# Rotation tables queued behind low weight parts and traced later, state-space and first score products a turn or two later, and the norms' rows loaded a unit ahead, in a one-core hybrid decoder step

## The chip, the cores and the metric

The kernel runs on one core of one Trainium2 chip. The number that counts is the device time of one execution in microseconds (us). Each kernel is timed as the median of several runs.

A core has five engines with queues of their own: PE (TensorE, matmuls; its weight loads are listed as PEld), DVE (VectorE), ACT (ScalarE), POOL (GpSimd) and SP (SyncE, which here only issues DMAs). Each engine works through its own list of instructions in the order in which the program put them there. Engines wait for each other by semaphores, and an instruction that waits holds up everything behind it in its own list.

## The reference, cut to what matters

One layer of a decoder: 528 prompt tokens (16 meta tokens and 512 more) and 8 sample tokens go through the same weights, in float32.

```python
xn = rmsnorm(x, norm_gain)
h = xn @ w_in                                  # 2048 x 8704
q, k, v, z_a, u, z_s, g_a, g_s = split(h)
q, k = rope(rmsnorm(q)), rope(rmsnorm(k))      # 16 query heads, 4 key heads of 64
o_a = sink_attention(q, k, v)                  # window 128, 16 meta keys, a sink
lam_bar = exp(lam * dt)                        # S5: complex diagonal, 64 groups x 64 states
b_bar = (lam_bar - 1) / lam * (b_re + i b_im)
h_t = lam_bar * h_(t-1) + b_bar u_t            # scan over time
y = gelu(Re(c h) + d_skip * u)
y = y * sigmoid(y @ w_glu + b_glu)
x + (sigmoid(g_a) * ((o_a * silu(z_a)) @ w_attn_out)
     + sigmoid(g_s) * ((y * silu(z_s)) @ w_ssm_out)) @ w_out
```

The new key and value windows and the final states are returned too.

## The kernel before, in words

**Weights.** A float32 product is made of three passes with shortened operands. Every weight tile `raw` of 128x1024 is loaded by SP, cut by ACT into a high part `whi` and by DVE into a low part `wlo = raw - whi`. PE then multiplies `whi` by the high and by the low part of the activations, and `wlo` by the high part. A low part that is late therefore stops PE.

**Stages, in the order of PE.** First come nine blocks of the input projection, taken as plain products (`mm`, line 1172). Sixteen quads follow: `Quads` and `quad` form two output blocks from seven products instead of eight, on sums and differences of weight tiles (`raw`, line 1077) and of activations (`tau`), with their products at line 1395 and their low parts at line 1079. A quad ends with DVE adding the last bank at line 1445. Quads 9 to 12, counted from 0, give the query heads. They go through `heads`, which writes each head block to DRAM as it is and with swapped halves (`rawD`, ten DMAs a quad). Then come the blocks listed in `ORDER1` (keys, values and the state-space input `u`), the rest of the gates, two plain stages (`w_glu` and the state-space output), the attention output, and eight quads for `w_out`.

**What runs beside them.** `Background` holds generators in three lanes. After a few matmuls the tracing code calls `step(budget)`. A generator then runs on to its next `yield`. `yield c` charges a cost `c` against the budget, and `yield None` ends that lane's turn. So a larger cost, or one more `yield None`, means that what follows is traced later in the program. In the quads a step comes after each of the seven products, with a budget of 0.5 (`GBUDGET`).

**What sets an engine's order.** The program is traced in one order, and a list scheduler then places each instruction on its engine by a model of its own. A low-priority instruction that looks ready early in that model may be placed well ahead of where it was traced. `with tc.issue_after(ins)` forbids this: every instruction traced inside it *on the engine of `ins`* comes after `ins`. `later()` is `issue_after(bg.last)`, where `bg.last` is the last product's final matmul. It binds the PE instructions traced inside and leaves DVE ones free.

**The rotation tables.** `ssm_prep` computes from `a`, `b` and `dt` on POOL some 200 small instructions (powers of the discretised eigenvalues, tables `T6` and `T11`). Then for each of eight unit blocks DVE makes a table out of `T11` and `T6` by four multiplications (line 308) and two combinations (lines 310 and 311), in one working buffer (`work`, the program's `room`). SP writes it to DRAM in two halves (`tabD`, line 314). The first two multiplications of the next table overwrite the half that is being written out, so they wait until those DMAs have landed.

**The state-space blocks.** `ssm_consts` loads and scales one block's constants and forms its `kp` products (line 410). `ssm_block` forms the `bu` products (line 471), scans on DVE, and forms the output products (lines 527 and 530).

**Norms of the heads.** `head_norms` takes the sums of squares that `heads` wrote to DRAM (`skD`, `sqD`), turns them into reciprocal roots on DVE and writes them back (`rkD`, `rqD`). `normed` lets the attention generator start, which also stands in lane 0 behind the eight state-space blocks.

**Attention.** It runs beside the last gates and the two plain stages: values, keys, then for each of four key heads the queries (`QT`, line 793) and four blocks of scores (line 809), softmax, transposes and weighing (line 858). The sample tokens' part ends at line 928, and `split` (lines 1678 and 1679) makes `A2` of it, which the attention output multiplies.

Of the kernel before, what the change touches and what calls it, by code (L numbers as in the profile page):

```python
# [146 lines left out]
    return r  # L147


def ssm_prep(nc, K, tmp, psum, dram, R, ident, a_prm, later, room):  # L150

    v = OnPool(nc, tmp)
    prm = K["prm"]
# [12 lines left out]
    v_.reciprocal(out=m2, in_=m2)  # L166
    dt = tmp.tile([P, 32], F32, name="dt")
    acc_exp(v, tmp, dt, ldt, 32)
    yield 1.6
    x = tmp.tile([P, 32], F32, name="xr")  # L170
    v.tensor_tensor(out=x, in0=are, in1=dt, op=ALU.mult)
    rho = tmp.tile([P, 32], F32, name="rho")
    acc_exp(v, tmp, rho, x, 32)
    th = tmp.tile([P, 32], F32, name="th")
    v.tensor_tensor(out=th, in0=aim, in1=dt, op=ALU.mult)
    yield 1.6

    magic = 12582912.0
    n = tmp.tile([P, 2, 32], F32, name="sc_n")
# [27 lines left out]
    v.tensor_tensor(out=e1, in0=r, in1=s, op=ALU.mult)  # L207
    lam = K["lam"]
    v.tensor_tensor(out=lam, in0=e1, in1=bc(rho, 1, 2), op=ALU.mult)
    yield 1.6  # L210

    g = tmp.tile([P, 2, 32], F32, name="f_g")
    v.tensor_scalar(out=g[:, 0], in0=lam[:, 0], scalar1=1.0, scalar2=None, op0=ALU.subtract)
# [13 lines left out]
    cmul(v, tmp, fv[:, :, 1:4], bc(fv[:, :, 0], 2, 3), lamp[:, 0, 0:3], lamp[:, 1, 0:3], (3, 32), "c96_")  # L227
    nF = K["nF"]
    v.tensor_scalar(out=nF, in0=fv[:, :, 0], scalar1=-1.0, scalar2=None, op0=ALU.mult)
    yield 1.3  # L230

    r4 = K["r4"]
    v.tensor_tensor(out=r4, in0=rho, in1=rho, op=ALU.mult)
# [12 lines left out]
    def powers(tab, z, cnt, tag):  # L246

        v.memset(tab[:, 0, :, 0], 1.0)
        v.memset(tab[:, 1, :, 0], 0.0)
        zs = [z]  # L250
        for i in range(3):
            nz = tmp.tile([P, 2, 32], F32, name=f"{tag}z{i}")
            cmul(v, tmp, nz, zs[-1], zs[-1][:, 0], zs[-1][:, 1], (32,), "c32_")
            zs.append(nz)
        n = 1
        for zp in zs:
            m = min(n, cnt - n)
            if m <= 0:
                break
            cmul(v, tmp, tab[:, :, :, n:n + m], tab[:, :, :, 0:m],  # L260
                 bc(zp[:, 0], 2, m), bc(zp[:, 1], 2, m), (32, m), "ct")
            n += m
            yield 0.8
        norm(tab, (32, cnt), "nt")
        yield 1.0
        return zs

    z = e1
# [13 lines left out]
    norm(c2, (32,), "n32")  # L282
    car = K["car"]
    v.tensor_tensor(out=car, in0=c2, in1=bc(r4, 1, 2), op=ALU.mult)
    yield 0.5
    for _ in range(14):
        yield None
    ft = psum.tile([P, 512], F32, name="tr")
    fts = tmp.tile([P, 2, P], F32, name="fts")
# [12 lines left out]
    t = [f.rearrange("p (r a i j) -> p r a i j", r=2, a=4, j=6) for f in (room[:, 0:8 * L], room[:, 8 * L:16 * L])]  # L302
    for ub in range(8):
        ps = slice(4 * ub, 4 * ub + 4)
        with later():
            for r in range(2):
                for e in range(2):
                    v_.tensor_tensor(out=t[r][:, e], in0=bc(T11[:, e, ps], 3, 6), in1=bc(T6[:, r, ps], 2, 11), op=ALU.mult)
            a, b = (f.rearrange("p r a i j -> p r (a i j)") for f in t)
            v_.tensor_tensor(out=a[:, 0], in0=a[:, 0], in1=b[:, 1], op=ALU.subtract)  # L310
            v_.scalar_tensor_tensor(out=a[:, 1], in0=a[:, 1], scalar=-1.0, in1=b[:, 0], op0=ALU.mult, op1=ALU.subtract)
            d = R["tabD"][ub].rearrange("p (x r l) -> p x r l", r=2, l=L)
            for r in range(2):
                nc.sync.dma_start(out=d[:, :, r], in_=t[0].rearrange("p r a i j -> p (r a) (i j)"))
        yield 2.4
# [23 lines left out]
def ssm_consts(nc, pool, dram, R, D, ub, a_bT, a_bN, a_cT, e32, d_skip, later, free):  # L339
# [64 lines left out]
    yield None  # L404

    kp = R["kp"]
    with later():
        for a in range(4):
            for i in range(2):
                nc.tensor.matmul(kp[32 * a:32 * a + 32, 0:P], lhsT=bb[:, a, i], rhs=CL[:, a, i, 0:4],  # L410
                                 start=(i == 0), stop=(i == 1))
# [34 lines left out]
def ssm_block(nc, pool, R, D, ub, y_out, later):  # L446
# [11 lines left out]
    tab = D["tab"]  # L458

    bu = R["bu"]  # L460

    def place(h, i, e):
        if (h, i) == (1, 0):
# [474 lines left out]
BUDGET2, BUDGET3, BUDGET4 = 6.0, 3.4, 4.8  # L938
HIGH = 4000
NLOAD = 3  # L940
NDELAY = 1
ATTC = (("kg", 1), ("kgs", 1), ("qg", 1), ("qgs", 1), ("mown", P), ("mprev", P), ("bd64", 4), ("sink", 16))
NXR = 10
NWARM = 9
# [85 lines left out]
class Quads:  # L1030
# [29 lines left out]
    def make(self, r):  # L1060
        nc = self.nc
        q, s = divmod(r, 7)
        if self.LOADS[s] is not None:
            self.load(4 * q + self.LOADS[s] + 4)
        if r < 7 and self.fourth:
            s = (0, 1, 2, 5, 3, 4, 6)[s]
        t = self.raw[4 * q + self.SRC[s]]
        pool, bufs = (self.pool, 3) if r % (3 + self.mp) < 3 else (self.more, self.mp)
        hi = pool.tile([P, 8, P], F32R, name="whi", bufs=bufs)
        lo = pool.tile([P, 8, P], F32R, name="wlo", bufs=bufs)  # L1070
        with self.tc.high_priority(offset=HIGH):
            for oi in self.SUMS[s]:
                if r < 7 and self.fourth and oi == (2, 0):
                    nc.gpsimd.dma_start(out=self.raw[2], in_=self.w[self.first], accum_op=ALU.add)
                    continue
                o, i = (self.raw[4 * q + j] for j in oi)
                nc.vector.tensor_tensor(out=o, in0=o, in1=i, op=ALU.add)  # L1077
            nc.scalar.copy(out=hi, in_=t)  # L1078
            nc.vector.tensor_tensor(out=lo, in0=t, in1=hi.bitcast(F32), op=ALU.subtract)  # L1079
        self.parts[r] = hi, lo  # L1080

    def upto(self, n):
# [10 lines left out]
def trunk(tc, A, O):  # L1093
# [62 lines left out]
        yield  # L1156


    pend, normed = [], []

    def mm(n, hi_of, lo_of, w0, budget=None, after=None, pool=None, name=None):

        ps = pool.tile([P, 2, 512], F32, name=name) if pool else mmp.tile([P, 2, 512], F32, name="mm")
        W = CH - w0
        for h in range(n):
            wh, wl = ws.get()
            for k in range(8):
                kt = 8 * h + k
                first, last = kt == 0, kt == 8 * n - 1
                for (wt, xo, f, l) in ((wh, hi_of, first, False), (wh, lo_of, False, False), (wl, hi_of, False, last)):  # L1170
                    for c in range(2):
                        m = nc.tensor.matmul(ps[:, c, 0:W], lhsT=wt[:, k], rhs=xo(kt, c), start=f, stop=l)  # L1172
                if k % grain[0] == grain[0] - 1:
                    bg.last = m.ins
                    bg.after = (ws.dve,) if at is not None else ()
                    bg.step((bud[0] if budget is None else budget) * grain[0] / 8)
            while pend and h == 0:
                pend.pop(0)()
            if after:
                after(h)  # L1180
        return ps[:, :, 0:W]
# [190 lines left out]
            pend.append(sums)  # L1372

    def head_norms():
        for src, dst, p, n in ((skD, rkD, 67, 32), (sqD, rqD, P, 65)):
            r1 = ev.tile([p, n], F32, name="z")
            r2 = ev.tile([p, n], F32, name="z")
            flat2 = lambda t: t.rearrange("a b -> (a b)").rearrange("(p n) -> p n", n=n)
            nc.sync.dma_start(out=r1, in_=flat2(src))
            v.tensor_scalar(out=r1, in0=r1, scalar1=1.0 / 64, scalar2=1e-6, op0=ALU.mult, op1=ALU.add)  # L1380
            rsqrt_dve(nc, ev, r2, r1, [p, n], "t", "")
            nc.sync.dma_start(out=flat2(dst), in_=r2)

    smp = []

# [113 lines left out]
    def xpart(k, c):  # L1499
# [4 lines left out]
    S = {}  # L1504
    flats = [xp.tile([P, 8 * CH], F32, name="work", tag=n) for n in ("xhq", "xlq")]
    bg.add(ssm_prep(nc, kept(flats[0][:, 0:NMADE], MADE), Places([flats[1], flats[0][:, NMADE:]], spots()), aux, dram, S,
                    C["idn"], A["prm"], lambda: tc.issue_after(bg.last), flats[1]))
    kD = dram.tile([P, NKEPT], F32, name="kept")

    def again():  # L1510
# [60 lines left out]
    for n_, (kind, n) in enumerate(ORDER1):  # L1571
# [4 lines left out]
        if kind == "h":  # L1576
            heads(n)
            if n == 3:
                pend.extend((head_norms, lambda: normed.append(1)))
            continue  # L1580
        if sp is None:
            spool = tc.tile_pool(name="ssm", bufs=2, side="right")
# [392 lines left out]
```

## Time and profile before

| | us |
|---|---|
| median of 3 runs | 1309.17 (1308.14 to 1310.37) |
| the profiled execution's own time | 1310.21 |
| its span in the profile | 1308.4 |
| PE busy | 1251.1 (96%) |
| DVE busy | 977.7 (75%) |
| ACT busy | 632.4 (48%) |
| POOL busy | 216.1 (17%) |

The granted TensorE clock was 0.986 on average over the span. HBM moved 226.75 MB, 173 GB/s on average. A row of the list of waits says which engine and line stood still, for what, for how long in total, how often, and how long at most. A row of the timeline gives start, duration, engine, line, operation, and in brackets the idle time before it with what ended that.

### The profile page before, as it was taken

What the parts mean: (1) busy time and instruction counts of PE and PEld (TensorE: products, weight loads), DVE (VectorE), ACT (ScalarE), POOL (GpSimd) and SP (SyncE); (2) the same over time, 40 slices, a digit from 0 to 9 for tenths busy, and PEclk for the clock granted to TensorE, in tenths of its full rate; (3) what the DMA queues carried; (4) which work ended last, traced back from release to release, by engine and by line L of the source; (5) the groups of instructions that cost most, each with busy time, mean ns of one, the idle gap of its engine ahead of it and who ended that gap; (6) DMA issues with size and microseconds to landing.
All of it is one profiled execution on the core that took longest, in us unless ns stands there. A gap on an engine that the chain in (4) does not pass through costs nothing.

```text
span 1308.4 us, 26458 instructions
## 1 busy us (share of the span) xinstructions
PE 1251.1 (96%) x10333; PEld 1226.8 (94%) x10333; DVE 977.7 (75%) x1516; ACT 632.4 (48%) x1351; POOL 216.1 (17%) x437
## 2 busy tenths in 40 slices
PE   9999982989999999999999998999999999999998
PEld 9999982979999999999999998989999999999998
DVE  8587843879778765777888857898995557787875
ACT  8553530435453539656653233667666323343442
POOL 0004997000000012222322122120010000000000
PEclk9999995999999999999999998999999999999999
DMA  8554331775355447666656479676676565464441
GB/s 286 196 172 147 116 128 30 153 177 153 128 160 162 149 144 225 186 201 182 176 158 185 123 223 258 187 246 212 191 229 219 188 202 181 147 220 153 154 138 50
DMA packets 125728, 226.75 MB, mean 173 GB/s; under 512 B 38700, under 2 KB 64260, under 8 KB 125572
## 3 DMA queue, kind: packets, MB, share of 16 engines
q1 hardware_dynamic: 116964, 206.63, 51.7%
q0 software_dynamic: 8640, 18.45, 5.7%
q8 instruction: 81, 1.33, 0.4%
q14 instruction: 43, 0.35, 0.1%
HBM read 185.34 MB, written 40.59 MB: 173 GB/s over the span
## 4 chain that ended last, share of the span: by engine, by line
PE 63%; DMA 12%; DVE 9%; POOL 8%; ACT 5%; issue 3%; SPq 2%; DVEq 0%; ACTq 0%; POOLq 0%
PE mm L1172 31%; PE pr L1395 27%; DMA tabD<-work 3%; ACT ct L362 2%; DMA xr<-in_x 1%; PE wg L858 1%; DMA sbw<-rawD 1%; DVE wlo L1013 1%; DMA c<-in_cT 1%; DMA raw<-in_w 1%; DMA bN<-in_bN 1%; POOL work L63 1%; ACT whi L1012 1%; POOL work L62 1%; POOL work L75 1%
## 5 line engine op out<-in xcount | busy, mean ns | idle before, releaser
L1078 ACT CAST whi<-raw 128x1024 fp32r<-128x1024 f32 x168 | 173.1, 1048 | 204.3 <-DVE raw L1077 121.0
L1079 DVE TENSOR_TENSOR wlo<-raw,whi 128x1024 fp32r<-128x1024 f32 x168 | 202.7, 1225 | 62.3 <-ACT whi L1078 61.9
L1395 PE MATMUL pr<-tau,whi 128*128 128x260 f32 x992 | 181.8, 285 | 1.7 <-DVE t L1430 1.0
L1172 PE MATMUL mm<-xh,whi 128*128 128x260 f32 (+1 forms) x744 | 173.6, 287 | 1.3 <-ACT xr L1232 1.3
L1172 PE MATMUL mm<-xh,wlo 128*128 128x260 f32 (+1 forms) x744 | 174.2, 287 | 0.0
L1172 PE MATMUL mm<-xl,whi 128*128 128x260 f32 (+1 forms) x744 | 173.3, 286 | 0.0
L1012 ACT CAST whi<-raw 128x1024 fp32r<-128x1024 f32 (+3 forms) x124 | 118.1, 962 | 111.1 <-PE mm L1172 68.1
L1013 DVE TENSOR_TENSOR wlo<-raw,whi 128x1024 fp32r<-128x1024 f32 (+3 forms) x124 | 137.5, 1117 | 34.9 <-ACT whi L1012 34.1
L1395 PEld LDWEIGHTS pr<-tau,whi 128*128 128x128 f32 x992 | 154.0, 190 | 2.2 <-DVE t L1430 1.3
L1395 PE MATMUL pr<-cb,whi 128*128 128x260 f32 x848 | 153.0, 283 | 0.0
L1395 PE MATMUL pr<-tau,wlo 128*128 128x260 f32 x496 | 140.7, 284 | 4.8 <-DVE wlo L1079 4.8
L1395 PE MATMUL pr<-xh,wlo 128*128 128x260 f32 x376 | 105.4, 285 | 31.4 <-DVE wlo L1079 31.4
L1395 PEld LDWEIGHTS pr<-cb,whi 128*128 128x128 f32 x848 | 130.8, 188 | 0.2 <-ACT z L1429 0.2
L1172 PEld LDWEIGHTS mm<-xh,whi 128*128 128x128 f32 x744 | 124.0, 189 | 2.5 <-ACT xr L1232 1.5
L1172 PEld LDWEIGHTS mm<-xh,wlo 128*128 128x128 f32 x744 | 124.2, 189 | 0.8 <-issue 0.8
L1172 PEld LDWEIGHTS mm<-xl,whi 128*128 128x128 f32 x744 | 124.7, 189 | 0.2 <-issue 0.2
L1395 PE MATMUL pr<-cb,wlo 128*128 128x260 f32 x424 | 119.1, 283 | 0.2 <-DVE wlo L1079 0.2
L1077 DVE TENSOR_TENSOR raw<-raw 128x1024 f32<-128x1024 f32 x95 | 116.3, 1225 | 1.3
L1395 PE MATMUL pr<-xl,whi 128*128 128x260 f32 x376 | 105.7, 284 | 0.0
L1395 PE MATMUL pr<-xh,whi 128*128 128x260 f32 x376 | 105.5, 285 | 0.0
L1172 PE MATMUL mm<-Y,whi 128*128 128x260 f32 x576 | 104.9, 287 | 0.3 <-DVE Y L1679 0.3
L1395 PEld LDWEIGHTS pr<-xh,wlo 128*128 128x128 f32 x376 | 70.6, 190 | 32.0 <-DVE wlo L1079 32.0
(426 smaller groups left out, 2937.6 us busy)
## 6 DMA issues: line engine op xcount, KB each, us to landing
raw<-in_w SPq DMA_DIRECT2D x202, 512.0 KB, 4.3
gD<-z SPq DMA_DIRECT2D x36, 260.0 KB, 3.6
t<-gD SPq DMA_DIRECT2D x32, 260.0 KB, 2.9
cache<-in_vc POOLq DMA_DIRECT2D x16, 286.0 KB, 3.5
cache<-in_kc POOLq DMA_DIRECT2D x15, 288.0 KB, 3.5
xr<-in_x SPq DMA_DIRECT2D x16, 268.0 KB, 4.3
xg<-in_x SPq DMA_DIRECT2D x8, 536.0 KB, 5.4
tabD<-work SPq DMA_DIRECT2D x16, 264.0 KB, 6.9
```

The costliest lines, as they stand in the source:

```text
L62: v.tensor_tensor(out=q, in0=q, in1=r, op=ALU.mult)
L63: v.tensor_scalar(out=q, in0=q, scalar1=cf[i], scalar2=None, op0=ALU.add)
L75: v.tensor_tensor(out=t1, in0=a, in1=bc(br, 1, 2), op=ALU.mult)
L362: nc.scalar.activation(out=dst, in_=src, func=AF.Copy, scale=x)
L858: nc.tensor.matmul(pv[64 * e:64 * e + 64, 0:256], lhsT=V, rhs=pr[:, e::2], start=(i == 0), stop=(i == len(parts) - 1))
L1012: nc.scalar.copy(out=hi, in_=raw)
L1013: self.dve = nc.vector.tensor_tensor(out=lo, in0=raw, in1=hi.bitcast(F32), op=ALU.subtract).ins
L1077: nc.vector.tensor_tensor(out=o, in0=o, in1=i, op=ALU.add)
L1078: nc.scalar.copy(out=hi, in_=t)
L1079: nc.vector.tensor_tensor(out=lo, in0=t, in1=hi.bitcast(F32), op=ALU.subtract)
L1172: m = nc.tensor.matmul(ps[:, c, 0:W], lhsT=wt[:, k], rhs=xo(kt, c), start=f, stop=l)
L1395: m = nc.tensor.matmul(bank, lhsT=wt[:, p], rhs=x(p, e), start=first and f and p == 0, stop=l and p == 7, skip_group_check=not first and l ...
```

## The change

Four things are edited.

1. **Rotation tables.** The table instructions are traced under `behind()` in place of `later()`. `behind()` is `issue_after(qs.dve)`, and `qs.dve` is the last low weight part that the quads have traced, which is a DVE instruction. The costs that `ssm_prep` charges on its way are nearly doubled (1.6 to 3.0, 1.3 to 2.5, 0.8 to 1.5, 1.0 to 2.0, 0.5 to 1.0), and its pause of 14 turns ahead of the transposes becomes one of 8.
2. **State-space products.** One more `yield None` stands ahead of the `kp` products and one ahead of the `bu` products.
3. **First scores.** `NDELAY`, the turns between the first queries and the first scores, goes from 1 to 3.
4. **Norms.** `head_norms` issues both row loads at once, into tiles named `t`. The arithmetic and the write-back move into `finish`, which runs after the second half of the same unit and behind the last low part. `normed` is set there.

```diff
-def ssm_prep(nc, K, tmp, psum, dram, R, ident, a_prm, later, room):
+def ssm_prep(nc, K, tmp, psum, dram, R, ident, a_prm, later, behind, room):
...
-    yield 1.6
+    yield 3.0
...
-            yield 0.8
+            yield 1.5
         norm(tab, (32, cnt), "nt")
-        yield 1.0
+        yield 2.0
...
-    yield 0.5
-    for _ in range(14):
+    yield 1.0
+    for _ in range(8):
         yield None
...
     for ub in range(8):
         ps = slice(4 * ub, 4 * ub + 4)
-        with later():
+        with behind():
...
     kp = R["kp"]
+    yield None
     with later():
...
     bu = R["bu"]
+    yield None
...
-NDELAY = 1
+NDELAY = 3
...
-            nc.vector.tensor_tensor(out=lo, in0=t, in1=hi.bitcast(F32), op=ALU.subtract)
+            self.dve = nc.vector.tensor_tensor(out=lo, in0=t, in1=hi.bitcast(F32), op=ALU.subtract).ins
...
             while pend and h == 0:
-                pend.pop(0)()
+                then.append(pend.pop(0)())
+            while then and h == 1:
+                f = then.pop(0)
+                if f:
+                    with tc.issue_after(ws.dve):
+                        f()
...
     def head_norms():
+
+        flat2 = lambda t, n: t.rearrange("a b -> (a b)").rearrange("(p n) -> p n", n=n)
+        rows = []
         for src, dst, p, n in ((skD, rkD, 67, 32), (sqD, rqD, P, 65)):
-            r1 = ev.tile([p, n], F32, name="z")
-            r2 = ev.tile([p, n], F32, name="z")
-            flat2 = lambda t: t.rearrange("a b -> (a b)").rearrange("(p n) -> p n", n=n)
-            nc.sync.dma_start(out=r1, in_=flat2(src))
-            v.tensor_scalar(out=r1, in0=r1, scalar1=1.0 / 64, scalar2=1e-6, op0=ALU.mult, op1=ALU.add)
-            rsqrt_dve(nc, ev, r2, r1, [p, n], "t", "")
-            nc.sync.dma_start(out=flat2(dst), in_=r2)
+            rows.append((ev.tile([p, n], F32, name="t"), dst, p, n))
+            nc.sync.dma_start(out=rows[-1][0], in_=flat2(src, n))
+
+        def finish():
+            for r1, dst, p, n in rows:
+                r2 = ev.tile([p, n], F32, name="z")
+                v.tensor_scalar(out=r1, in0=r1, scalar1=1.0 / 64, scalar2=1e-6, op0=ALU.mult, op1=ALU.add)
+                rsqrt_dve(nc, ev, r2, r1, [p, n], "z", "")
+                nc.sync.dma_start(out=flat2(dst, n), in_=r2)
+            normed.append(1)
+
+        return finish
...
-                    C["idn"], A["prm"], lambda: tc.issue_after(bg.last), flats[1]))
+                    C["idn"], A["prm"], lambda: tc.issue_after(bg.last), lambda: tc.issue_after(qs.dve), flats[1]))
...
-                pend.extend((head_norms, lambda: normed.append(1)))
+                pend.append(head_norms)
```

How this moves instructions, at three places on which the prediction rests. `work` is the working buffer of the tables, `tabD` their place in DRAM, `sbw` the loaded query or key rows, `QT` the finished queries, and `wlo` and `raw` the weights as above.

Place 1 is DVE around the first table in the quads. Before (the second to last row is the second table's first pair):

```order
L1204 TENSOR_TENSOR z<-z,R 128x520
L1079 TENSOR_TENSOR wlo<-raw,whi 128x1024 x3
L308 TENSOR_TENSOR work<-work 128x264 x4
L1079 TENSOR_TENSOR wlo<-raw,whi 128x1024
L311 SCALAR_TENSOR_TENSOR work<-work 128x264
L310 TENSOR_TENSOR work<-work 128x264
L1079 TENSOR_TENSOR wlo<-raw,whi 128x1024
L308 TENSOR_TENSOR work<-work 128x264 x2
L1077 TENSOR_TENSOR raw<-raw 128x1024
```

After the change:

```order
L1460 TENSOR_TENSOR z<-z,pr_3525 128x520
L1079 TENSOR_TENSOR raw<-raw 128x1024
L1211 TENSOR_TENSOR z<-z,R 128x520
L1081 TENSOR_TENSOR wlo<-raw,whi 128x1024 x2
L308 TENSOR_TENSOR work<-work 128x264 x4
L1081 TENSOR_TENSOR wlo<-raw,whi 128x1024
L311 SCALAR_TENSOR_TENSOR work<-work 128x264
L310 TENSOR_TENSOR work<-work 128x264
L1081 TENSOR_TENSOR wlo<-raw,whi 128x1024
L308 TENSOR_TENSOR work<-work 128x264 x2
```

The neighbours are alike, but the place is another one. Before, the third quad's last bank (line 1445) was the last one added ahead of the first table. Now it is the ninth quad's (the row L1460 here). The other seven tables, which stood beside quads 3 to 6, stand beside quads 9 to 12, and the eighth comes as quad 12 ends.

Place 2 is DVE ahead of the first queries. Before, `z<-mm` at line 1204 being the eviction of a gate block:

```order
L1204 TENSOR_TENSOR z<-mm,R 128x520
L1013 TENSOR_TENSOR wlo<-raw,whi 128x1024
L753 TENSOR_TENSOR KL_9016<-sbw,KH_9012 64x4x64 x2
L753 TENSOR_TENSOR KL_9016<-sbw,KH_9012 64x4x16
L753 TENSOR_TENSOR KL_9017<-sbw,KH_9013 64x4x64 x2
L753 TENSOR_TENSOR KL_9017<-sbw,KH_9013 64x4x16
L716 SCALAR_TENSOR_TENSOR sbw<-sbw,k_attc 128x520
L717 SCALAR_TENSOR_TENSOR sbw<-sbw,k_attc 128x520
L719 TENSOR_TENSOR sbw<-sbw 128x520
L725 TENSOR_TENSOR sbw<-sbw,rb 128x4x64 x2
L1013 TENSOR_TENSOR wlo<-raw,whi 128x1024
L793 TENSOR_TENSOR QT_9359<-sbw,QT_9359 64x512
```

After the change:

```order
L718 SCALAR_TENSOR_TENSOR sbw<-sbw,k_attc 128x520
L719 SCALAR_TENSOR_TENSOR sbw<-sbw,k_attc 128x520
L1211 TENSOR_TENSOR z<-mm,R 128x520
L721 TENSOR_TENSOR sbw<-sbw 128x520
L1015 TENSOR_TENSOR wlo<-raw,whi 128x1024
L718 SCALAR_TENSOR_TENSOR sbw<-sbw,k_attc 128x520
L727 TENSOR_TENSOR sbw<-sbw,rb 128x4x64 x2
L719 SCALAR_TENSOR_TENSOR sbw<-sbw,k_attc 128x520
L795 TENSOR_TENSOR QT_9526<-sbw,QT_9526 64x512
```

On PE the first scores stand 98 matmuls behind the end of that evicted block before, and 96 behind it now. The first pair's two multiplications that wait for a load (lines 716 and 717, now 718 and 719) have moved ahead of the eviction. The second pair's have come ahead of the first `QT`.

Place 3 is SP's queue in the head quads, after the change, from the third table's halves to the fifth's:

```order
L314 DMA tabD<-work 1024x1x66 x2
L1058 DMA raw<-in_w 128x1024
L314 DMA tabD<-work 1024x1x66 x2
L1058 DMA raw<-in_w 128x1024
L1345 DMA rawD<-z 256x1x260
L1351 DMA rawD<-z 64x1x260 x4
L1376 DMA sqD<-z 2x2x260 x2
L314 DMA tabD<-work 1024x1x66
L1058 DMA raw<-in_w 128x1024
L314 DMA tabD<-work 1024x1x66
```

Before, the same sixteen `tabD` DMAs shared the queue with weight loads and two gate writes a quad. Now they share it with weight loads and the heads' ten `rawD` writes a quad, and the two halves of the fifth and eighth tables have a weight load between them.

More of the change, by code (lines that the diff above doesn't have):

```diff
@@ L175, in ssm_prep @@
     v.tensor_tensor(out=th, in0=aim, in1=dt, op=ALU.mult)
-    yield 1.6
+    yield 3.0
     magic = 12582912.0
@@ L229, in ssm_prep @@
     v.tensor_scalar(out=nF, in0=fv[:, :, 0], scalar1=-1.0, scalar2=None, op0=ALU.mult)
-    yield 1.3
+    yield 2.5
     r4 = K["r4"]
@@ L1156, in xkeep @@
         yield
-    pend, normed = [], []
+    pend, then, normed = [], [], []
     def mm(n, hi_of, lo_of, w0, budget=None, after=None, pool=None, name=None):
```

2 lines of the change are left out of this document (1 added, 1 removed).

## The prediction

> **What bounds the kernel now.** I read the page's shares first, then the rows by slices, then the waits, the windows around the one hole in PE, and the timeline there.
>
> ```profile
> PE 1251.1 (96%) x10333; PEld 1226.8 (94%) x10333; DVE 977.7 (75%) x1516; ACT 632.4 (48%) x1351; POOL 216.1 (17%) x437
> PE   9999982989999999999999998999999999999998
> PEclk9999995999999999999999998999999999999999
> ```
>
> PE is the bound: it stands for 57 of the 1308.4 us. The seventh slice (196 to 229 us) is nearly empty, and its clock has dropped. PE's own waits between 220 and 300 us:
>
> ```profile
> PE pr L1395 <- DVE wlo L1079: 36.1, 5, 29.2
> PE pr L1395 <- DVE t L1430: 1.0, 1, 1.0
> PE pr L1395 <- ACT whi L1078: 0.7, 1, 0.7
> ```
>
> That is 37.8 us of waiting, nearly all for low weight parts. The waits of all engines tell why DVE did not deliver them, and the timeline shows the place:
>
> ```profile
> DVE work L308 <- POOL work L244: 34.7, 1, 34.7
> DVE work L308 <- DMA tabD<-work: 12.9, 7, 3.2
> ...
> 179.79 3.70 DVE L1079 TENSOR_TENSOR wlo<-raw,whi 128x1024 fp32r<-128x1024 f32 x3 [0.52 <-ACT whi L1078]
> 218.21 1.71 DVE L308 TENSOR_TENSOR work<-work 128x264 f32<-128x264 f32 x4 [34.72 <-POOL work L244]
> 221.11 0.58 PE L1395 MATMUL pr<-xh,wlo 128*128 128x260 f32 x1 [29.21 <-DVE wlo L1079]
> ```
>
> DVE met the first table at 183.49 us, while POOL was still computing its input, and stood for 34.7 us with the low parts behind it. PE lived on what was finished until 221.11 - 29.21 = 191.90 us. So DVE's lead there was 191.90 - 183.49 = 8.4 us.
>
> **Part 1, the tables: what goes.** The 37.8 us above, and a slow clock after each hole. Windows (busy us and count of PE, PEld, DVE, ACT, POOL, then clock, DMA share, GB/s):
>
> ```profile
> 120.00:180.00 60.00, 60.00 (x502) 60.00 (x501) 49.80 (x51) 28.35 (x40) 55.94 (x85) 1.00 0.42 137
> 190.00:218.00 28.00, 1.91 (x16) 1.70 (x15) 0.00 (x0) 0.05 (x1) 27.77 (x83) 0.62 0.00 0
> 220.00:230.00 10.00, 7.88 (x53) 7.58 (x54) 9.30 (x15) 1.69 (x2) 0.40 (x1) 0.80 0.51 105
> 231.00:297.00 66.00, 58.31 (x461) 57.01 (x461) 53.72 (x80) 27.25 (x39) 0.00 (x0) 0.97 0.78 168
> 280.00:290.00 10.00, 7.76 (x52) 7.55 (x52) 7.21 (x13) 4.04 (x7) 0.00 (x0) 0.83 0.90 197
> 361.00:444.00 83.00, 83.00 (x700) 80.77 (x699) 63.38 (x64) 38.76 (x56) 0.00 (x0) 1.00 0.50 154
> ```
>
> At full clock a matmul takes 60.00 / 502 = 0.1195 us. The 53 of the third row should take 6.33 us and took 7.88, the 52 of the fifth 6.21 and took 7.76: 3.1 us together. What can go is 37.8 + 3.1 = 40.9 us.
>
> Does the first table now find its input? POOL's last input came 34.7 us after 183.49, at 218.2. The table now stands behind the ninth quad. Its last bank was added here:
>
> ```profile
> 340.94 0.70 DVE L1445 TENSOR_TENSOR z<-z,pr 128x520 f32<-128x520 f32 x1 [0.74 <-PE pr L1395]
> ```
>
> Without the 40.9 us that is 300 us, 82 us after POOL's end. But POOL will be slower: with DVE standing it did 83 instructions in 27.77 us (0.33 each), with DVE 83% busy 85 in 55.94 (0.66). The 83 at 0.66 take 55 us and end near 190 + 55 = 245. I keep 55 us in hand, and the 34.7 us wait is gone.
>
> **Part 1, what comes.** The tables now stand among quads 9 to 12. A pair of their instructions takes 0.77 us, so six take 2.3:
>
> ```profile
> 222.80 0.77 DVE L308 TENSOR_TENSOR work<-work 128x264 f32<-128x264 f32 x2
> ```
>
> Each later table also waits for the previous one's DMA, 12.9 / 7 = 1.84 us on average, 3.2 at most. Did PE suffer from that before? In the window 231 to 297 DVE was busy for 53.72 us and stood some 12 us for these DMAs, which fills the 66 us: DVE set PE's pace there, with no lead left. Its waits of 1 to 3 us cost PE 66 - 58.31 = 7.7 us.
>
> In quads 9 to 12 (the window 361 to 444, four quads) DVE has 83 - 63.38 = 19.6 us to spare, 4.9 a quad. Five tables fall on the first two quads: 5 x 2.3 + 4 x 1.84 = 18.9 us, against 2 x 4.9 of slack and 8.4 of lead: 0.7 us too much. With the longest wait it is 5 x 2.3 + 4 x 3.2 = 24.3, and 6.1 too much. The other three spread over two quads and fit. The new cost for PE lies between 0 (the lead holds) and 9 (7.7 as at no lead, and 1.5 of slow clock). I take 3, the middle of 0.7 and 6.1: the case is nearer to the row with a lead, but SP has more to issue there.
>
> That SP queue: each head quad issues ten `rawD` writes ahead of or between the tables' halves.
>
> ```profile
> 358.57 0.53 SPq L1338 DMA_DIRECT2D rawD<-t  x1
> 364.19 3.12 SPq L1344 DMA_DIRECT2D rawD<-t  x4
> ```
>
> One head block holds SP for 0.53 + 3.12, some 3.6 us. Behind SP's waiting table halves stand weight loads. These run up to a quad ahead, so I cost them nothing; without that cover they are the rival below. Part 1 gives 40.9 - 3 = 37.9 us.
>
> **Parts 2 and 3, products and scores later.** PE's own waits again:
>
> ```profile
> PE aux L809 <- DVE QT L793: 6.0, 1, 6.0
> PE tr L471 <- DVE g L544: 1.7, 1, 1.7
> PE tr L530 <- DVE H L516: 1.3, 1, 1.3
> PE aux L410 <- ACT z L1365: 0.8, 1, 0.8
> ...
> 793.10 0.76 DVE L716 SCALAR_TENSOR_TENSOR sbw<-sbw,k_attc 128x520 f32<-128x520 f32 x1 [3.51 <-DMA sbw<-rawD]
> 796.52 0.76 DVE L717 SCALAR_TENSOR_TENSOR sbw<-sbw,k_attc 128x520 f32<-128x520 f32 x1 [2.67 <-DMA sbw<-rawD]
> ```
>
> The 6.0 us at the first scores are the 3.51 + 2.67 = 6.2 that DVE stood for two query loads, between the eviction of a gate block and the first `QT`. In the new order this pair stands ahead of the eviction, with about as many matmuls from there to the scores. But the second pair's two loads now precede the first `QT`. So the gain is 6.0 if they have landed and 0 if they bring the same wait. I take 4.5, since these loads have one block (96 matmuls, 11.5 us) more to land in than the first pair had.
>
> The later `kp` and `bu` products can save 0.8 + 1.7 = 2.5 us. All blocks behind them also move, so a new wait of that size is as likely; the 1.3 at line 530 shows what such a one costs. I take 0, from -3 (loss) to 2.5.
>
> The attention ends later: in the new order its last weighing stands 189 matmuls ahead of the attention output, before 286. Those 97 are 11.7 us. The spare before:
>
> ```profile
> 1027.80 1.30 DVE L1679 TENSOR_TENSOR A<-oT,A 128x520 fp32r<-128x520 f32 x2
> 1050.08 0.64 PE L1172 MATMUL mm<-A,whi 128*128 128x260 f32 x4
> ```
>
> 21.0 us lie between the last part and its first use, so 9.3 remain: no cost. Past that cover every us of delay would be one of PE's.
>
> **Part 4, the norms.**
>
> ```profile
> 616.18 0.18 DVE L1380 TENSOR_SCALAR z<-z 67x32 f32<-67x32 f32 x1 [1.66 <-DMA z<-skD]
> ```
>
> DVE's 1.66 us go, but PE has no wait there (its lead hides it), so I count 0. The write-back and `normed` come half a block later. The attention stands behind the last state-space block in its lane anyway, and so this is hidden; uncovered it would cost the same 1.7.
>
> **Sum.** 37.9 + 4.5 + 0 + 0 = 42.4 us off the profiled execution's 1310.2 gives 1267.8. The median of the runs is 1.0 lower: 1309.2 - 42.4 = 1266.8, say 1267. With all gains at their best end (40.9 + 6.0 + 2.5 = 49.4) it is 1260, at their worst (40.9 - 9 + 0 - 3 = 28.9) 1280.
>
> **Rivals.**
>
> *SP lengthens the table loop.* If each table's halves stand behind one head block, each of the seven waits becomes 1.84 + 3.6 = 5.4 us. Eight tables then hold DVE for 8 x 2.3 + 7 x 5.4 = 56 us, against 19.6 of slack and 8.4 of lead: PE loses 28. The gain is 40.9 - 28 + 4.5 = 17.4, the time 1292. For it: ten `rawD` writes a quad share the queue. Against: the last three tables have ten and more DVE instructions between them, and the heads write in bursts of one block.
>
> *POOL is late after all.* In the Trainium skill, "SBUF — State Buffer", section "SBUF: two separate sides", DVE and GpSimd share a port pair that one instruction holds to its end while the other fully blocks. This case's 0.33 against 0.66 us agrees. By that rule taken to its end every POOL instruction could wait for a whole DVE one. As a mechanism from rows: 3.70 / 3 = 1.23 us on each of 83 makes 83 x (0.33 + 1.23) = 130 us, and POOL ends at 320. DVE then stands 20 us at the first table, less the 8.4 of lead: 12 us for PE, time 1279. Against: under full load the row shows 0.66.
>
> *Slower than before: the table loop as a chain of DMA and queue.* Place: SP in quads 9 to 12, where two tables have a weight load between their halves that itself waits for DVE. Break-even is where PE loses 40.9 + 4.5 = 45.4: 8 x 2.3 + 7 h - 28 = 45.4, so h = 7.9 us of DVE standing per table. SP's own waits have a row of this kind:
>
> ```profile
> SPq L1056 <- DVE raw L1077: 15.6, 5, 7.9
> ```
>
> With h = 1.84 + 7.9 = 9.7 PE loses 58, and the time is 1309 - 45 + 58 = 1322. Against: only two tables of eight are split so, and h never passed 3.2.
>
> That the change does not do what it says is excluded by the order: no table stands ahead of the ninth quad's end.
>
> **Chances.** Forecast 0.80 (1267, own range 1260 to 1280), SP 0.12 (1292), POOL 0.04 (1279), slower 0.04 (1322). No change is taken as within 0.2% (2.6 us), about what runs of this kernel can tell apart; only the upper end of the SP case comes near it, 0.01. So faster has 0.95, same 0.01, slower 0.04. The range for 8 in 10: 1258 to 1287, the forecast's and POOL's case and part of the SP case.
>
> **What would show it.** Right: no POOL wait on line 308; PE waits for line 1081's low parts (1079 before) between the first quad and the last under 9 us; POOL's small instructions ending between 235 and 260 us; the clock row without its 5; the wait at the first scores under 3 us; the last split ahead of the attention output by 5 to 15 us. Wrong: waits of more than 3.5 us on `tabD` in quads 9 to 12 with PE gaps behind them (SP's case), a wait on POOL near 300 us, new waits over 3 us in the state-space stage, or a hole ahead of the attention output.

## The result and the profile after

The changed kernel took 1273.41 us (median of 4 runs, 1270.12 to 1277.01), the kernel before 1308.66 us beside it. The ratio is 0.9732, 95% interval 0.9701 to 0.9762. That is 35.3 us off; 42.4 were forecast, and 1267 us. The profiled execution took 1277.01 us, the longest of the four.

The page's shares and rows by slices of the change, to be laid beside those of before:

```profile
PE 1254.0 (98%) x10333; PEld 1229.2 (96%) x10333; DVE 983.8 (77%) x1516; ACT 632.1 (50%) x1351; POOL 267.0 (21%) x437
PE   9999999999899999999999999999999999999998
PEclk9999999999899999989999998999999999999999
```

The empty slice and the 5 in the clock row are gone. What is new is an 8 in the eleventh slice, which is 319 to 351 us, the first quads that give query heads. PE's own waits:

```profile
PE pr L1410 <- DVE z L1445: 5.1, 1, 5.1
PE aux L811 <- DVE QT L795: 3.1, 2, 2.4
PE tr L532 <- DVE H L518: 2.9, 1, 2.9
PE pr L1410 <- DVE t L1445: 1.6, 1, 1.6
...
PE pr L1410 <- DVE wlo L1081: 0.2, 1, 0.2
```

The 36.1 us for low parts have become 0.2. In their place PE waits 5.1 + 1.6 us for line 1445. That is not the last bank of a quad (line 1445 before, 1460 now) but the first addition, line 1430 before: DVE adds bank `b` to a first result, and only then may the quad's last product overwrite that bank. The prediction listed a wait of this kind, 1.0 us for line 1430, but gave it no place in the new cost. DVE's waits at the tables:

```profile
DVE work L308 <- DMA tabD<-work: 15.7, 5, 6.6
```

No wait for POOL is left on that line. The waits for the write-out are fewer (5, before 7), but longer. DVE's timeline around the longest:

```profile
331.99 1.23 DVE L1079 TENSOR_TENSOR raw<-raw 128x1024 f32<-128x1024 f32 x1
339.82 0.78 DVE L308 TENSOR_TENSOR work<-work 128x264 f32<-128x264 f32 x2 [6.60 <-DMA tabD<-work]
340.51 1.22 DVE L1079 TENSOR_TENSOR raw<-raw 128x1024 f32<-128x1024 f32 x1
341.65 0.43 DVE L310 TENSOR_TENSOR work<-work 128x264 f32<-128x264 f32 x1
341.99 0.43 DVE L311 SCALAR_TENSOR_TENSOR work<-work 128x264 f32<-128x264 f32 x1
342.33 0.42 DVE L1450 TENSOR_TENSOR z<-z,pr 128x260 f32<-128x260 f32 x1
342.67 1.22 DVE L1081 TENSOR_TENSOR wlo<-raw,whi 128x1024 fp32r<-128x1024 f32 x1
343.80 0.42 DVE L1445 TENSOR_TENSOR z<-z,pr 128x260 f32<-128x260 f32 x1
...
344.28 0.80 PE L1410 MATMUL pr<-tau,whi 128*128 128x260 f32 x2 [5.08 <-DVE z L1445]
```

DVE stood for 6.6 us, and the bank's add came only after six more rows, 4.0 us later. PE resumed right behind it. The chain of waits, which gives start, duration and what, shows how long the write-outs themselves took:

```profile
306.30 7.00 DMA tabD<-work
...
316.92 7.11 DMA tabD<-work
...
329.70 10.03 DMA tabD<-work
...
343.02 6.94 DMA tabD<-work
...
355.96 8.59 DMA tabD<-work
```

The same view of before had such rows too, and the prediction did not use them:

```profile
222.51 6.35 DMA tabD<-work
...
232.15 8.12 DMA tabD<-work
...
243.50 7.08 DMA tabD<-work
```

So a table's write-out takes 6 to 8 us in before and 7 to 10 in the change, from the start of the second half's transfer to the release of DVE. The wait of 1.84 us, from which the prediction reckoned, is only what was left of it after DVE had done other work meanwhile.

**Where the time went.** I compared the start of the n-th weight product (lines 1172 and 1395 before, 1174 and 1410 now) in the two traces. Both hold 9024 of them.

| weight product | before, us | change ahead by, us |
|---|---|---|
| 1200 | 188.6 | 0.2 |
| 1800 | 303.8 | 43.2 |
| 2400 | 376.7 | 43.1 |
| 2600 | 401.5 | 33.1 |
| 3200 | 475.2 | 32.4 |
| 4000 | 589.9 | 27.6 |
| 9000 | 1301.6 | 33.2 |

The hole gave 43.1 us. The head quads took 10.7 of them back. Behind them 4.8 were lost in the state-space blocks, at the wait for `H` shown above, and 5.6 gained later. The 33.2 at the end is the difference of the two spans, 1308.4 - 1275.2.

### The profile page after: what moved, and what is told of

Its sections match the earlier page's. It is cut to its first block, busy times and chain, and to the rows that moved or that the text cites. A ratio compares the mean times of both kernels' runs of the same rounds, so it can differ in the third digit from the quotient of the medians.

```text
span 1275.2 us, 26461 instructions
## 1 busy us (share of the span) xinstructions
PE 1254.0 (98%) x10333; PEld 1229.2 (96%) x10333; DVE 983.8 (77%) x1516; ACT 632.1 (50%) x1351; POOL 267.0 (21%) x437
## 4 chain that ended last, share of the span: by engine, by line
PE 81%; DMA 9%; DVE 5%; issue 2%; SPq 2%; ACT 1%; POOL 0%; DVEq 0%; POOLq 0%; ACTq 0%
PE mm L1174 39%; PE pr L1410 32%; DMA tabD<-work 3%; PE wg L860 2%; DMA sbw<-rawD 1%; PE aux L1410 1%; DMA xr<-in_x 1%; PE aux L1174 1%; DMA raw<-in_w 1%; DMA U<-uD 1%; PE aux L811 1%; PE aux L812 1%; DMA yD<-g 1%; PE mm L1731 1%; PE tr L842 1%
## 5 line engine op out<-in xcount | busy, mean ns | idle before, releaser
L1081 DVE TENSOR_TENSOR wlo<-raw,whi 128x1024 fp32r<-128x1024 f32 x168 | 206.8, 1252 | 57.8 <-ACT whi L1080 57.5
L1079 DVE TENSOR_TENSOR raw<-raw 128x1024 f32<-128x1024 f32 x95 | 119.0, 1253 | 1.5
L1410 PEld LDWEIGHTS pr<-tau,wlo 128*128 128x128 f32 x496 | 94.1, 190 | 0.0
```

The source lines that it names most:

```text
L1081: self.dve = nc.vector.tensor_tensor(out=lo, in0=t, in1=hi.bitcast(F32), op=ALU.subtract).ins
L1410: m = nc.tensor.matmul(bank, lhsT=wt[:, p], rhs=x(p, e), start=first and f and p == 0, stop=l and p == 7, skip_group_check=not first and l ...
```

## Experiments

The kernel before had medians of 1308.66, 1303.65, 1308.16 and 1304.09 us beside the four sets of runs. So times are compared within a set, and across sets by ratios, or by the number of us by which the n-th product stands ahead.

### Which half of part 1 removes the hole

`p234_alone` is the change with part 1 undone. `queue_old` has the new costs without the queueing. `costs_old` has the queueing with the old costs.

```diff
 # p234_alone: both of the following; queue_old: the first; costs_old: the second
-        with behind():
+        with later():
...
-    yield 3.0        # and the other costs of ssm_prep
+    yield 1.6
...
-    for _ in range(8):
+    for _ in range(14):
```

> The change without its first part: tables queued and costed as before, parts 2, 3 and 4 as in the change. The prediction's terms for these parts are 4.5 us (first scores) and 0: by them 1308.7 - 4.5 = 1304.2 us, between 1300 and 1312. The rival comes from the two traces: in the change's trace the weight products ahead of the state-space blocks run 32.3 us earlier than before and those behind the attention 31.8 us earlier, so parts 2 to 4 bring nothing: 1308 to 1309 us, the same as before.

> The change with its tables again free on DVE (later in place of behind), all new costs kept. If the queueing behind the low parts is what removes the hole, the tables stand in the fourth quad again (they do by the order), DVE reaches the first one near 185 us and waits for POOL some 30 to 35 us as before: 1302 to 1312 us. If the new costs alone did it, the time would be that of the change, 1273 us, and no POOL wait on line 308 over 3 us.

> The change with the old costs and the pause of 14 turns, tables still queued behind low parts. The first table then stands behind the sixth quad, which ends near 237 us, while POOL ended at 266 in the change. At 0.76 us each some 38 POOL instructions are left at 237 us; with DVE standing they take 0.33, 12.5 us. Less DVE's lead of about 8 us PE loses 3 to 8 us there, and the tables' transfers cost in quads 6 to 9 the 7 to 11 us they cost elsewhere: 1274 to 1282 us if the tables cost PE the same wherever they crowd. If only the head quads make them dear (their ten extra writes), the half of the tables that stands ahead of quad 9 is cheap, and the time is 1268 to 1274.

| | us | ratio to before | interval |
|---|---|---|---|
| before | 1303.65 | | |
| p234_alone | 1300.48 | 0.9975 | 0.9965 to 0.9986 |
| queue_old | 1301.71 | 0.9979 | 0.9966 to 0.9993 |
| costs_old | 1277.68 | 0.9804 | 0.9785 to 0.9822 |

DVE's waits at the tables in `queue_old`:

```profile
DVE work L308 <- POOL work L244: 34.7, 1, 34.7
DVE work L308 <- DMA tabD<-work: 10.3, 6, 3.3
```

The wait for POOL is back to the tenth of a us. Traced later but free on DVE, the tables are put into the fourth quad again, so the new costs alone bring nothing: with parts 2 to 4 in it, this run is 1.9 us below before, and 0.3 us below the 1302 to 1312 expected. The queueing alone brings most of it; `costs_old` then waits in this place:

```profile
252.10 1.72 DVE L308 TENSOR_TENSOR work<-work 128x264 f32<-128x264 f32 x4 [8.89 <-POOL work L244]
```

By products, `costs_old` is 36.3 us ahead at product 1600, as the change is. At 2400 it is 26.2 ahead, where the change has 43.1, and it loses nothing in the head quads. Its 1277.7 lies in the branch where crowded tables cost PE about the same in any quad. That is no clean answer, since 8.9 us for POOL are mixed in. The costs are there to get past POOL's end.

In `p234_alone` parts 2 to 4 bring 3.2 us (1.8 to 4.6). The rival that they bring nothing falls: up to the last table DVE's instructions and SP's DMAs stand in the same order as in before, so the 3.2 are not a matter of where the tables stand.

### What makes the head quads dear

`tables_spread` takes the crowd away. A pause of `yield None` lets credit pile up to a cap of 3.0, which then releases two tables at once. A cost does not.

```diff
-    for _ in range(8):
-        yield None
+    for _ in range(1):
+        yield 3.0
...
-        yield 2.4
+        yield 3.2
```

> The change with one table a quad: the pause of 8 turns becomes one cost of 3.0, so that no credit piles up, and a table costs 3.2 in place of 2.4. The eight tables then stand whole behind the quads 9 to 16, counted from 1, with no half of the next one among them. Theory: the 11.3 us that PE loses between 325 and 410 us in the change (its weight products go from 43.1 us ahead of before to 31.8) come from tables that crowd, so that DVE stands for the write-out of the one before. Then no wait for tabD is left, and all 11 us come back: 1273.4 - 11 = 1262 us, 1260 to 1265. Rival: any table among the head quads is dear, because its own instructions and SP's added writes delay evictions there: PE keeps 4 us or more of waits in 300 to 440 us and the time is 1267 to 1274.

It took 1257.83 us, ratio 0.9646 (0.9632 to 0.9660), less than the 1260 to 1265 that was expected. In a second set it took 1257.98 beside the unaltered change:

> The change itself once more, unaltered, as the base for the other runs beside it: 0.970 to 0.976 of the time before, and again 5 to 12 us of PE lost between 325 and 410 us, with DVE waits for tabD of over 3.5 us there. If that loss was a chance of the one profiled execution, the waits for tabD stay under 3.3 us and the time is that of the run with one table a quad plus at most 5 us.

> The change with one table a quad, once more, as the base for the two runs that undo a part of it: 0.963 to 0.966 of the time before, no DVE wait for tabD.

| | us | ratio to before | interval |
|---|---|---|---|
| before | 1308.16 | | |
| change_again | 1271.09 | 0.9712 | 0.9696 to 0.9729 |
| spread_again | 1257.98 | 0.9612 | 0.9595 to 0.9629 |

Windows from 300 to 440 us (busy us and count of PE, PEld, DVE, ACT, POOL, then clock, DMA share, GB/s) of `change_again`, then of `spread_again`:

```profile
300.00:440.00 140.00, 133.02 (x1081) 129.25 (x1080) 114.92 (x156) 64.01 (x95) 0.00 (x0) 0.98 0.70 163
```

```profile
300.00:440.00 140.00, 140.00 (x1174) 137.77 (x1173) 119.66 (x156) 67.42 (x99) 2.10 (x3) 1.00 0.72 177
```

With one table a quad PE never stands there and the clock is full. The change does 93 matmuls fewer, 11.1 us at 0.1195. Of that PE stood 140 - 133.02 = 7.0 us, and 133.02 - 1081 x 0.1195 = 3.8 are slow clock. DVE does the same 156 instructions in both. In neither run with spread tables does DVE wait for `tabD` at line 308. The loss was no chance of one execution: `change_again` has DVE waits of 16.2 us in 5 and loses 11.2 in the head quads. The rival that tables are dear among heads in any place falls. This version is 13 us faster than the change, and the fastest kernel of this study; by products some 3 of the 13 come behind the head quads.

The second ratio lies just under what was expected, and the two of this one kernel, 0.9646 and 0.9612, have intervals that do not touch. Its times are 0.15 us apart: it is the kernel before that differs, by 4.5 us. So ratios from different sets are comparable to some 0.4% only. The traces show one place where crowded tables take different times. In the first of these two sets `p234_alone`, with before's order, has write-outs of 5.8 to 7.1 us in the chain of waits, and at product 1800 it is 5.2 us ahead of the kept trace of before, which has 6.4 to 8.1. With spread tables no wait is left that could depend on it.

Is it the writes queued ahead, SP's queue, or the crowd? `heads_on_pool` issues the heads' `rawD` writes on POOL, `tables_on_pool` the tables' write-outs. `pause_kept` and `rate_kept` each undo one half of `tables_spread`.

```diff
 # heads_on_pool, at both rawD writes
-        nc.sync.dma_start(out=rawD[i]...
+        (nc.sync if i < 4 else nc.gpsimd).dma_start(out=rawD[i]...
 # tables_on_pool
-                nc.sync.dma_start(out=d[:, :, r], ...
+                nc.gpsimd.dma_start(out=d[:, :, r], ...
 # pause_kept: the change with only this
-        yield 2.4
+        yield 3.2
 # rate_kept: the change with only this
-    for _ in range(8):
-        yield None
+    for _ in range(1):
+        yield 3.0
```

> The change with the query heads' ten rawD writes a quad issued by POOL in place of SP, tables as in the change. In the change the write-out of a table that stood behind these writes and two weight loads landed 9.5 us after its issue (329.08 + 1.28 to 339.82), against 5.8 to 7.1 in before. If the bytes queued ahead of it on SP's queue are what made the waits long, no wait for tabD passes 3.5 us, PE loses under 6 us between 325 and 410 us, and the time is 1262 to 1266 (change 1271). If it is the crowding alone, landing times and waits stay as they are and the time is 1268 to 1273.

> The change with the tables' write-outs issued by POOL in place of SP. POOL has nothing else to do there, so SP's order plays no part. If SP's queue made the waits long, they fall under 3.5 us and the time is 1262 to 1266. If the write-out itself (two writes of 1024 short packets) takes 6 us or more from issue to landing wherever it is queued, DVE still stands for it where tables crowd, and the time stays at 1267 to 1273.

> The change with a table's cost at 3.2 but with the pause of 8 turns, in which credit piles up: three tables then crowd behind quad 9 and the rest come nearly one a quad. If the crowd at the start makes the loss, PE loses 3 us or more and the time is 1261 to 1268. If the rate over the first two quads decides (five tables in the change, three here), DVE's waits stay at the 1.2 and 1.9 us of the change's first two, PE loses 0 to 2 us, and the time is 1258 to 1260.

> The change without the pause's piled-up credit but with a table's cost at 2.4: about three tables in two quads from the start, two pairs of them close together. If the crowd at the start makes the loss, nothing is lost: 1258 to 1260 us. If the rate does, DVE waits over 3 us for tabD at the close pairs and PE loses 3 us or more: 1261 to 1268.

The last three columns: us ahead of before at products 2400 and 3200, and the longest DVE wait for `tabD`.

| | us | ratio | interval | at 2400 | at 3200 | wait |
|---|---|---|---|---|---|---|
| change_again (other set) | 1271.09 | 0.9712 | 0.9696 to 0.9729 | 43.1 | 31.9 | 6.6 |
| heads_on_pool | 1267.14 | 0.9720 | 0.9700 to 0.9739 | 43.0 | 37.1 | 4.7 |
| tables_on_pool | 1264.74 | 0.9700 | 0.9683 to 0.9716 | 43.1 | 40.3 | 2.2 |
| rate_kept | 1260.12 | 0.9667 | 0.9646 to 0.9688 | 42.8 | 41.3 | 1.3 |
| pause_kept | 1259.34 | 0.9658 | 0.9641 to 0.9674 | 42.1 | 41.4 | 0.9 |
| spread_again (other set) | 1257.98 | 0.9612 | 0.9595 to 0.9629 | 43.1 | 43.1 | none |

With the heads' writes off SP, the loss in the head quads falls from 11.2 to 5.9 us by the trace. The loss is that of the case against the heads' writes, but a wait of 4.7 us is left, and the time lies between the two cases. The ratio cannot be told from the change's. DVE's timeline and the chain of waits of `heads_on_pool`:

```profile
335.72 0.78 DVE L308 TENSOR_TENSOR work<-work 128x264 f32<-128x264 f32 x2 [2.48 <-DMA tabD<-work]
...
359.33 0.78 DVE L308 TENSOR_TENSOR work<-work 128x264 f32<-128x264 f32 x2 [4.71 <-DMA tabD<-work]
```

```profile
327.30 8.40 DMA tabD<-work
```

With the write-outs off SP the loss is 2.7 us, and waits and time came out as expected for the case that SP's queue made the waits long. But the write-outs are hardly shorter, which was expected for the other case. The chain of `tables_on_pool`:

```profile
306.66 5.82 DMA tabD<-work
...
327.52 9.22 DMA tabD<-work
...
341.12 7.56 DMA tabD<-work
...
352.36 6.62 DMA tabD<-work
```

So SP's queue is not what makes the write-outs long. SP adds the time until a finished table is issued, behind weight loads and the heads' writes: in the change 1.2 us for the third table (327.86 to 329.08) and 2.4 for the second half of the fifth (353.60 to 355.96). The Trainium skill, "DMA: Bandwidth & Descriptors", section "Issuing engines are not separate DMA queues", says that transfers of all issuing engines run on the same 16 DMA engines and interleave, and that another issuer saves only time on the sequencer. These rows agree: 5.8 to 9.2 us from POOL, 6.9 to 10.0 from SP.

`pause_kept` and `rate_kept` each give nearly all back: each came out as expected for the case that the other half does the harm, `rate_kept` 0.1 us above it. So neither the burst nor the rate does it alone. What they share with `spread_again` shows in DVE's timelines, when two times are taken from them: the time between a table's last row and the overwriting pair of the next without DVE's wait for `tabD`, and, where DVE waited, the whole time between these two.

| | time between, without the wait, us | whole time where DVE waited, us |
|---|---|---|
| before | 4.4 to 7.6 | 7.2 to 8.8 (7 waits) |
| change | 5.4 to 7.0 at the waits, else 9.4 and 11.5 | 7.6, 7.8, 7.8, 11.0, 12.0 |
| heads_on_pool | 5.6 to 6.6 at the waits | 6.9, 6.9, 7.4, 9.1, 10.5 |
| tables_on_pool | 6.4 to 8.4 at the waits | 7.0, 7.8, 8.7, 9.2, 10.4 |
| rate_kept | 6.5 to 15.7 | 7.7, 7.9, 7.9 |
| pause_kept | 6.6 to 16.8 | 7.5 |
| spread_again | 8.0 to 20.1 | none |

The tables stand no closer together in the change than in before. But in the head quads a buffer comes free after up to 12.0 us, not after at most 8.8, and DVE's 5 to 7 us of other work no longer cover most of it. With the heads' writes or the write-outs moved off SP it is still up to 10.5, so more than SP's queue is at work. In `tables_on_pool` the scheduler also put a little more work between the tables, so how much of its gain is SP's, and which transfers slow the write-out, was not settled. Space between the tables makes it harmless.

### What parts 2 and 3 are worth

Both were undone on the version with spread tables, whose runs lie close together.

```diff
 # spread_scores_old
-NDELAY = 3
+NDELAY = 1
 # spread_products_old
     kp = R["kp"]
-    yield None
...
     bu = R["bu"]
-    yield None
```

> The change with one table a quad and part 3 undone (NDELAY 1). By the prediction part 3 is worth 4.5 us (0 to 6): the time is 4.5 us above that of the run with one table a quad, and PE's wait at the first scores is 6 us again. By the traces taken so far the first-scores place gains about 5 us and the end of the attention gives some 2 back: 3 us above. Rival: the wait merely moves, 0 to 1 us above.

> The change with one table a quad and part 2 undone (the added turns ahead of the kp and bu products taken out). By the prediction part 2 is worth 0 (a loss of 3 to a gain of 2.5): within 2.5 us of the run with one table a quad. A theory from the change's trace, where PE lost some 4 us in the state-space blocks, 2.9 of them in one wait for the scan's H: part 2 costs, and without it the time is 2 to 4 us lower. The runs with other table orders, which keep part 2 and show 2 to 5 us gained in that stage, speak against it.

`spread_scores_old` took 1260.81 us, 2.8 more than `spread_again`; its ratio is 0.9635 (0.9619 to 0.9651). `spread_products_old` took 1263.17, 5.2 more, beyond the 2.5 that the prediction allowed; 0.9655 (0.9639 to 0.9672). PE's waits at the first scores with both parts, without part 3, and without part 2:

```profile
PE aux L811 <- DVE QT L795: 3.5, 2, 2.5
```

```profile
PE aux L811 <- DVE QT L795: 5.6, 1, 5.6
```

```profile
PE aux L811 <- DVE QT L795: 5.7, 1, 5.7
```

Each part alone leaves the old wait of nearly 6 us; only both together bring it down. With part 2 undone the attention starts earlier (first `QT` at 752.1 us, with it at 758.8), and the two turns of part 3 no longer suffice. The granted clock there falls further too, as windows around this wait show, with both parts and then without part 2:

```profile
745.00:775.00 30.00, 26.52 (x206) 26.09 (x205) 19.89 (x34) 11.81 (x25) 10.97 (x22) 0.94 0.85 245
```

```profile
740.00:770.00 30.00, 24.28 (x186) 24.07 (x185) 21.51 (x35) 8.44 (x12) 5.27 (x10) 0.89 0.88 253
```

In 30 us, 0.94 makes 1.8 us of slow clock and 0.89 makes 3.3. With the 2.2 us of longer waiting this place makes 3.7 of the 5.2. So part 2's worth comes mostly from here, and not from the waits for `kp` and `bu`, to which the prediction tied it. The theory that part 2 costs 2 to 4 us falls. Since both work on one wait, 2.8 and 5.2 should not be added.

The 2.9 us for `H` in the profiled execution of the change were a late transfer, not part 2: the other traces with part 2 have between none and 4.3 us of this wait. Window 530 to 550 of it, and ACT's timeline there:

```profile
530.00:550.00 20.00, 17.11 (x123) 16.03 (x123) 14.26 (x21) 12.44 (x44) 8.50 (x15) 0.83 0.72 195
```

```profile
532.58 5.61 ACT L362 ACTIVATE ct<-c,kept 128x64 f32<-128x64 f32 x23 [8.64 <-DMA c<-in_cT]
```

In `change_again` ACT stood 5.80 us for the same load, and PE did 167 matmuls there in place of 123. These 44 make 5.3 us, as much as lies between 1277.01 and the 1271.77 of that execution.

## Why the prediction was right and where it was not

**The hole goes, and why: right.** The 40.9 us of waits and slow clock were 43.1 by the trace. `queue_old` shows that the queueing does it, and `costs_old` that with the old costs the first table comes 8.9 us ahead of POOL's end.

**POOL's end: its size was off, without harm.** It was put at 245 us, 235 to 260; the last instruction ended at 265.8. From 190 to 260 us POOL did 92 instructions in 69.77, 0.76 each, not 0.66, with DVE 87% busy and not 83% as in the row I took:

```profile
190.00:260.00 70.00, 70.00 (x584) 70.00 (x584) 60.95 (x58) 31.30 (x44) 69.77 (x92) 1.00 0.37 125
```

The first table started at 302.27, so 36 us of cover were left.

**The new cost of the tables: this is the step that failed.** It was 3 us, 0 to 9, and measured 10.7 and 11.2. Two sizes in it were wrong. The waits were taken as 1.84 us each, the mean of a row (3.2 at most). But that is a small difference of two larger times, some 8 us until the buffer is free and some 6 of other work; where the first grew by 3 to 4, the wait grew by as much, and 15.7 us stand where 7.4 (12.8 with the longest) were assumed. In the prediction's own sum that makes 5 x 2.3 + 15.7 - 9.8 - 8.4 = 9.0 us of standing; PE stood 6.7 to 7.0. The slow clock was 3.6 to 3.8 us instead of 1.5. PE stopped for a bank and not for low parts: DVE frees PE's banks as well, and this work too was queued behind the table. The cover of 8.4 us, which is DVE's lead with low parts, says nothing of that. The window taken for quads 9 to 12 also lay one quad late, but nothing hangs on it: from 341 to 424 us DVE was busy for 63.67 us, not 63.38. That the time still fell into the range is in part luck: this term left its own range, and the hole gave 2.2 us more than was counted.

**The rival on SP.** It named the right place and mechanism (waits over 3.5 us on `tabD` with PE gaps behind them) at a third of its size: PE lost 11 and not 28. Only two of five waits passed 3.5 us, and with the write-outs off SP 2.7 us are still lost: SP has a share, and not the whole. The slower case fell with it: DVE stood 15.7 us in all, 2 a table, where 7.9 were needed.

**First scores: right, somewhat too large.** 4.5 (0 to 6) were forecast, 2.8 measured; the longest wait is 2.4 us, under 3 as named. DVE's timeline of the change:

```profile
771.48 0.76 DVE L718 SCALAR_TENSOR_TENSOR sbw<-sbw,k_attc 128x520 f32<-128x520 f32 x1 [7.36 <-DMA sbw<-rawD]
...
772.89 0.69 DVE L1211 TENSOR_TENSOR z<-mm,R 128x520 f32<-128x520 f32 x1
...
775.25 0.75 DVE L718 SCALAR_TENSOR_TENSOR sbw<-sbw,k_attc 128x520 f32<-128x520 f32 x1
...
777.37 0.69 DVE L795 TENSOR_TENSOR QT<-sbw,QT 64x512 fp32r<-64x512 f32 x1
```

The wait for the first pair's loads is still there, 7.36 us, but ahead of the eviction. The second pair's loads had landed, as was hoped. The 3.1 us that PE still waits come from DVE's own work between the eviction and `QT`, where no row waits.

**`kp` and `bu`: the term was mis-sized.** 0 (a loss of 3 to a gain of 2.5) against 5.2, mostly through the first scores, which the prediction treated apart.

**The attention's end: right.** 9.3 us of spare were forecast:

```profile
1007.64 0.69 DVE L1694 TENSOR_TENSOR A<-oT,A 128x520 fp32r<-128x520 f32 x1
```

```profile
1016.86 0.64 PE L1174 MATMUL mm<-A,whi 128*128 128x260 f32 x4
```

It is 1016.86 - 1008.33 = 8.5 us.

**The norms** were not undone apart, and what they bring stays open. PE has no wait there in either trace.

**The sum.** To the forecast of 42.4 the hole adds 2.2, and the tables' cost takes 8.0 (11.0 for 3). Parts 2 and 3 together are worth somewhere between the 3.2 of `p234_alone` and the 8.0 that the two undone runs would add up to, against 4.5. That gives 35.3 to 40.1; measured were 35.3 and, in the second set, 37.1.

## What to carry to other kernels

A wait in a list of waits is what is left of a transfer after the waiting engine's other work. When either is about to change, reckon with the transfer's whole length from the chain of waits, here 7 to 10 us and not 1.84, and lay the uses of one buffer farther apart than that. And look at how a planner saves credit: a pause that lets it pile up releases the next pieces in a burst.

## What the runs showed of the hardware that was not expected

**Two writes of 264 KB in short packets take 6 to 10 us** beside other traffic, whichever of two engines issues them (rows above).

**POOL's smallest instructions can take as long as one of DVE's.** The change's timeline of POOL, and of DVE beside it:

```profile
247.16 0.25 POOL L77 TENSOR_TENSOR work<-work 128x32 f32<-128x32 f32 x1
247.33 1.23 DVE L1081 TENSOR_TENSOR wlo<-raw,whi 128x1024 fp32r<-128x1024 f32 x1 [1.38 <-ACT whi L1080]
247.38 1.29 POOL L78 TENSOR_TENSOR work<-work 128x32 f32<-128x32 f32 x1
248.63 1.44 POOL L77 TENSOR_TENSOR work<-work 128x96 f32<-128x96 f32 x1
```

The same shape takes 0.25 us when it starts while DVE stands, and 1.29 beside a low part on DVE, which takes 1.23. The Trainium skill, "SBUF — State Buffer", section "SBUF: two separate sides", has the port pair held for a whole instruction, and these rows agree for single instructions. On the mean it was 0.76, not the 0.33 + 1.23 of the prediction's rival. Not every instruction of POOL met one of DVE's, as the first row shows.
